# An adding transfer in place of a vector sum: S1 of a seven-product weight chunk made by DMA in the raw buffer

## The chip, the core and the metric

The kernel runs on one core of one Trainium2 chip. The metric is the device time of one execution in microseconds. Engines are named as in the profile: PE (matrix products), PEld (its weight loads), DVE (vector), ACT (scalar), POOL (GpSimd) and SP (which only issues transfers here).

## The reference, cut to what matters

A two-layer decoder trunk on 512 tokens of width 1024. Each layer is a mixer between two half-step SwiGLU feed-forward blocks, so there are four feed-forward blocks in all:

```
def swiglu(h, w_gate, w_up, w_down):
    return (jax.nn.silu(h @ w_gate) * (h @ w_up)) @ w_down

for i in range(2):
    x = x + 0.5 * swiglu(rmsnorm(x, ffn1_norm[i]), ffn1_w_gate[i], ffn1_w_up[i], ffn1_w_down[i])
    x = x + mixer_i(rmsnorm(x, mix_norm[i]))          # gated linear attention, then stick-breaking attention
    x = x + 0.5 * swiglu(rmsnorm(x, ffn2_norm[i]), ffn2_w_gate[i], ffn2_w_up[i], ffn2_w_down[i])
return rmsnorm(x, final_norm)
```

w_gate and w_up are 1024 x 2816, w_down is 2816 x 1024, all in float32.

## The kernel before, in words

Activations lie with features on partitions, tokens along the free dimension. Every float32 factor is split into a high part rounded to fp32r and a low part that is the rest; a product is three matrix products, high x high, low x high and high x low. The split of a weight is one copy on ACT (L138) and one subtraction on DVE (L139), in `Entry.split`.

A feed-forward block walks over 11 chunks of 256 columns of w_gate and w_up. From the third chunk on (9 of w_gate and 9 of w_up in each block, 72 in all) a chunk is a "seven-product" chunk: its 1024 x 256 block is read as a 2 x 2 matrix of blocks and multiplied with the 2 x 2 blocks of the activations by Strassen-Winograd, in seven products of 12 matrix products each instead of eight. In the tile `t` of a raw chunk (128 x 8 x 256) the blocks are A11 = `t[:, 0:4, 0:P]`, A21 = `t[:, 0:4, P:]`, A12 = `t[:, 4:8, 0:P]`, A22 = `t[:, 4:8, P:]`. The weights need four sums:

- S1 = A21 + A22 (L704) and S2 = S1 − A11 (L705), made by `sums_12` in one tile of 1024 columns and split as one unit;
- S3 = A11 − A21 (L710) and S4 = A12 − S2 (L711), made by `sums_34` likewise.

A chunk has two entries in the feed's queue, `body_1` (products with A11, S1, S2 and A12) and `body_2` (S3, S4, A22). After the product with A11 ACT copies the result from ps_w to ps_z (L746), and only then may PE go on in ps_w. The results go out through ACT copies (L749, L752, L764), DVE sums (L765, L769) and the gate: for w_gate a Silu on ACT (L729), for w_up a product on DVE (L732).

`Feed.start` sets the order of the work: at each entry it splits up to three entries ahead (no more than four full-size units), makes the sums of up to four entries, and loads the chunks of up to six. A load (L105) is one transfer of 1 MB issued by SP into one of two "raw" buffers; it waits until the buffer's last reader is done. Loads of down weights (`rawd`) stand in the same SP queue. A sum is made when its entry comes into view, so the first reader of a raw chunk on DVE is S1. Each engine works its instructions off in the order in which they were written.

Between the seven-product chunks stand the down products: `down` (results ps_d, in part copied by ACT at L340 and added onto the residual by a POOL-issued adding transfer, x<-d, L341) and `seven_down` (L374 to L445, with its own sums S1 to S4 from `rawd`, its own copies into ps_z at L408 and its additions onto the residual at L396).

Of the kernel before, what the change touches and what calls it, by code (L numbers as in the profile page):

```python
# [10 lines left out]
F32 = mybir.dt.float32  # L11
# [4 lines left out]
ALU = mybir.AluOpType  # L16
PSUM = bass.MemoryType.PSUM

P = 128
T = 512  # L20
D = 1024
KD = D // P
# [8 lines left out]
def turns(t):  # L31

    return t.rearrange("p (two n) -> p n two", two=2)


def flat(ps):

    return ps.rearrange("p (n two) -> p two n", two=2)


def pair(t):

    return t.rearrange("p (two n) -> p two n", two=2)
# [3 lines left out]
def decoder(ctx: ExitStack, tc: tile.TileContext, a: dict, out: bass.AP):  # L47
    nc = tc.nc
# [12 lines left out]
    def psum(name, tag=None):  # L61
        if tag is None:
            tag = order[turn_[0] % 8]
            turn_[0] += 1
        return pp.tile([P, T], F32, tag=tag, bufs=banks[tag], name=name)
# [25 lines left out]
    class Chunk:  # L91
        def __init__(self, src, n, m):
            self.src, self.n, self.m, self.t = src, n, m, None
            self.pool = None
            self.few = False

        def load(self):
            if self.t is None:
                if self.pool is not None:
                    self.t = self.pool.tile([P, self.n, self.m], F32, tag="raw0", bufs=4, name="raw0")  # L100
                elif self.few:
                    self.t = st["few"].tile([P, self.n, self.m], F32, tag="rawd", bufs=2, name="rawd")
                else:
                    self.t = wp.tile([P, self.n, self.m], F32, tag="raw", bufs=2, name="raw")
                nc.sync.dma_start(self.t, self.src)  # L105
            return self.t

    class Entry:
# [504 lines left out]
    class FFN:  # L613
# [80 lines left out]
        def seven(self, ch, group=None):  # L694

            H = T // 2
            s12, v = [None], {}  # L700

            def sums_12(t):
                s = s12[0] = self.tp.tile([P, KD, P], F32, tag="s", bufs=4, name="s12")
                nc.vector.tensor_tensor(out=s[:, 0:4], in0=t[:, 0:4, P:], in1=t[:, 4:8, P:], op=ALU.add)  # L704
                nc.vector.tensor_tensor(out=s[:, 4:8], in0=s[:, 0:4], in1=t[:, 0:4, 0:P], op=ALU.subtract)  # L705
                return s

            def sums_34(t):
                s = self.tp.tile([P, KD, P], F32, tag="s", bufs=4, name="s34")
                nc.vector.tensor_tensor(out=s[:, 0:4], in0=t[:, 0:4, 0:P], in1=t[:, 0:4, P:], op=ALU.subtract)  # L710
                nc.vector.tensor_tensor(out=s[:, 4:8], in0=t[:, 4:8, 0:P], in1=s12[0][:, 4:8], op=ALU.subtract)  # L711
                return s

            def prod(o, w, w0, b, first=True, c0=0):
                for j in range(4):
                    bh, bl = (turns(t) for t in b(j))
                    wh, wl = (t[:, w0 + j, c0 : c0 + P] for t in w)
                    for n, (l_, r_) in enumerate(((wh, bh), (wl, bh), (wh, bl))):
                        st["pe"] = nc.tensor.matmul(  # L719
                            o, l_, r_, start=first and j + n == 0, stop=j == 3 and n == 2, skip_group_check=True  # L720
                        ).ins

            def half(k0, c):
                return lambda j: (st["h"][k0 + j][:, c * H : c * H + H], st["l"][k0 + j][:, c * H : c * H + H])

            def gate(o, c, t):

                if group is None:
                    st["silu"] = nc.scalar.activation(pair(o[:, c : c + H]), t, AF.Silu).ins  # L729
                else:  # L730
                    g = self.gates[0 if o is v["o"][0] else 1]
                    nc.vector.tensor_tensor(  # L732
                        out=pair(o[:, c : c + H]), in0=t, in1=pair(g[:, c : c + H]), op=ALU.mult
                    )

            def body_1(W):


                a11, s, a2 = W
                v["a2"] = a2  # L740
                v["w"], v["q"] = psum("ps_w"), psum("ps_q")
                z = psum("ps_z")[:, 0:H]
                w, q = (v[n][:, 0:H] for n in "wq")
                o0, o1 = v["o"] = [self.tp.tile([P, T], F32, tag="t", name=n) for n in ("o0", "o1")]
                prod(w, a11, 0, half(0, 0))
                nc.scalar.copy(z, w)  # L746
                yield
                prod(q, s, 0, lambda j: self.t_half(0, j))
                nc.scalar.copy(pair(o1[:, H:T]), flat(q))  # L749
                yield  # L750
                prod(w, s, 4, lambda j: self.t_half(1, j), first=False)
                nc.scalar.copy(pair(o0[:, H:T]), flat(w))  # L752
                yield
                prod(z, a2, 0, half(4, 0), first=False)
                gate(o0, 0, flat(z))
                yield

            def body_2(W):
                (s,) = W
                w, q = (v[n][:, 0:H] for n in "wq")  # L760
                o0, o1 = v["o"]
                prod(w, s, 0, lambda j: self.t_half(2, j), first=False)
                u3 = self.tp.tile([P, H], F32, tag="c", bufs=1, name="u3")
                nc.scalar.copy(pair(u3), flat(w))  # L764
                nc.vector.tensor_tensor(out=o1[:, H:T], in0=u3, in1=o1[:, H:T], op=ALU.add)  # L765
                yield
                prod(q, s, 4, half(4, 1), first=False)
                oh = pair(o0[:, H:T])
                nc.vector.tensor_tensor(out=oh, in0=flat(q), in1=oh, op=ALU.add)  # L769
                gate(o0, H, oh)  # L770
                if group is not None:
                    close_0(o0)
                gate(o1, H, pair(o1[:, H:T]))
                yield
                prod(w, v["a2"], 0, lambda j: self.t_half(3, j), first=False, c0=P)
                gate(o1, 0, flat(w))
                if group is not None:
                    close_1(o0, o1)
                    del self.gates[:2]
                else:  # L780
                    self.gates += [o0, o1]
                yield

            def close_0(o0):
                if group in self.DOWN_SEVEN:
                    self.close_first(o0, group)
                else:
                    self.close(o0, group)

            def close_1(o0, o1):  # L790
                if group in self.DOWN_SEVEN:
                    self.close_second(o0, o1, group)
                else:
                    self.close(o1, group)


            units = [(ch, lambda t: t[:, 0:4, 0:P], 4, P), (ch, sums_12, KD, P), (ch, lambda t: t[:, 4:8], 4, 256)]
            feed.q.append(Entry(units, body_1))
            feed.q.append(Entry([(ch, sums_34, KD, P)], body_2))

        def t_half(self, i, j):
# [1112 lines left out]
```

## Time and profile before

| | |
|---|---|
| median of 3 runs | 1779.24 us (1779.19 to 1779.93) |
| the profiled execution's own time | 1779.44 us |
| its span | 1777.5 us |
| PE, DVE, ACT, POOL busy | 1756.3, 1508.6, 1081.6, 58.4 us |
| granted clock of TensorE | 0.999 |
| DMA | 193.93 MB, mean 109 GB/s |

The profile is of one execution. Busy time is the union of an engine's instructions; a group of instructions is given as line, engine, operation, output<-inputs, shapes and count, then busy us in all and mean ns of one, and after the second bar the idle time of that engine just before them with what ended it. Matrix products overlap one another, so their mean duration is longer than their distance. A timeline row has start, duration, engine, line and operands. A DMA row ends with the median time from issue to landing.

### The profile page before, as it was taken

How to read it: one execution, taken by the hardware profiler on the slowest of the kernel's cores; microseconds unless marked ns; L12 is line 12 of the kernel's file. 1: busy time of each engine (PE TensorE's matmuls, PEld its weight loads, DVE VectorE, ACT ScalarE, POOL GpSimd, SP SyncE). 2: the span in 40 equal slices, each digit the busy share in tenths (PEclk: the TensorE clock that was granted, in tenths of full speed). 3: DMA queues.
4: the chain of work that ended last, by engine and by line, in shares of the span. 5: the costliest groups of instructions: out<-in, count | busy, mean ns of one | idle time of the engine just before them, and what ended most of it. 6: DMA issues, size and time to landing. Idle time of an engine off the chain costs nothing.

```text
span 1777.5 us, 31388 instructions
## 1 busy us (share of the span) xinstructions
PE 1756.3 (99%) x12714; PEld 1630.4 (92%) x12714; DVE 1508.6 (85%) x2471; ACT 1081.6 (61%) x1886; POOL 58.4 (3%) x80
## 2 busy tenths in 40 slices
PE   9999999999999999999999999999999999999998
PEld 8999999889888899999889999999888888999997
DVE  8999797786888989888798988967898679997985
ACT  7556556554655556555565555555889745665655
POOL 0000000200000000000000000010000000000000
PEclk9999999999999999999999999999999999999999
DMA  5543435422123433344424344342212134434342
GB/s 168 153 120 118 125 103 148 112 72 72 49 95 95 130 108 119 119 119 126 141 85 130 103 124 135 110 120 83 84 49 78 66 95 131 131 108 129 114 131 65
DMA packets 186820, 193.93 MB, mean 109 GB/s; under 512 B 4978, under 2 KB 171172, under 8 KB 186676
## 3 DMA queue, kind: packets, MB, share of 16 engines
q1 hardware_dynamic: 177760, 175.91, 31.7%
q0 software_dynamic: 8672, 15.74, 4.9%
q8 instruction: 99, 1.62, 0.4%
q14 instruction: 45, 0.37, 0.1%
q10 hardware_dynamic: 244, 0.29, 0.0%
HBM read 175.17 MB, written 2.10 MB: 100 GB/s over the span
## 4 chain that ended last, share of the span: by engine, by line
PE 67%; DVE 22%; ACT 5%; DMA 3%; issue 3%; POOL 0%; DVEq 0%; SPq 0%; ACTq 0%; POOLq 0%
PE ps_w L719 16%; PE ps_d L80 11%; PE ps_q L719 8%; PE ps_f L80 7%; DVE wl L139 5%; PE ps_t L80 4%; PE ps_z L719 4%; PE ps_w L390 4%; PE ps_b L80 3%; PE ps_q L390 2%; ACT wh L138 2%; DMA raw<-in_ffn_w_gate_dram 1%; DVE ts L826 1%; PE ps_z L1402 1%; DVE nl L817 1%
## 5 line engine op out<-in xcount | busy, mean ns | idle before, releaser
L139 DVE TENSOR_TENSOR wl<-raw,wh 128x1024 fp32r<-128x1024 f32 x241 | 255.0, 1059 | 59.8 <-ACT wh L138 59.1
L138 ACT CAST wh<-raw 128x1024 fp32r<-128x1024 f32 x241 | 221.7, 921 | 77.1 <-PE ps_f L80 22.6
L139 DVE TENSOR_TENSOR wl<-s,wh 128x1024 fp32r<-128x1024 f32 x176 | 214.3, 1218 | 47.2 <-ACT wh L138 47.2
L719 PE MATMUL ps_w<-th,wh 128*128 128x256 f32 x864 | 239.4, 277 | 4.2 <-ACT ps_z L746 4.1
L719 PE MATMUL ps_w<-th,wl 128*128 128x256 f32 x864 | 237.6, 275 | 0.0
L719 PE MATMUL ps_w<-tl,wh 128*128 128x256 f32 x864 | 237.6, 275 | 0.0
L138 ACT CAST wh<-s 128x1024 fp32r<-128x1024 f32 x176 | 184.1, 1046 | 69.1 <-DVE s L705 19.3
L719 PEld LDWEIGHTS ps_w<-th,wh 128*128 128x128 f32 x864 | 165.8, 192 | 7.6 <-ACT ps_z L746 7.6
L80 PE MATMUL ps_f<-xh,wh 128*128 128x512 f32 x432 | 166.4, 386 | 0.0
L719 PEld LDWEIGHTS ps_w<-tl,wh 128*128 128x128 f32 x864 | 165.9, 192 | 0.0
L719 PEld LDWEIGHTS ps_w<-th,wl 128*128 128x128 f32 x864 | 165.8, 192 | 0.0
L80 PE MATMUL ps_f<-xh,wl 128*128 128x512 f32 x432 | 164.2, 380 | 0.5 <-DVE wl L139 0.5
L80 PE MATMUL ps_f<-xl,wh 128*128 128x512 f32 x432 | 163.9, 379 | 0.0
L80 PE MATMUL ps_d<-hl,wh 128*128 128x512 f32 x416 | 158.0, 380 | 1.7 <-DVE hl L817 1.7
L80 PE MATMUL ps_d<-hh,wh 128*128 128x512 f32 x416 | 158.0, 380 | 0.5 <-ACT hh L816 0.5
L80 PE MATMUL ps_d<-hh,wl 128*128 128x512 f32 x416 | 157.7, 379 | 0.0
L139 DVE TENSOR_TENSOR wl<-rawd,wh 128x1024 fp32r<-128x1024 f32 (+1 forms) x100 | 96.0, 963 | 16.0 <-ACT wh L138 15.8
L138 ACT CAST wh<-rawd 128x1024 fp32r<-128x1024 f32 (+1 forms) x100 | 82.8, 845 | 39.3 <-PE ps_d L80 25.6
L341 POOL DMA_DIRECT2D x<-d x56 | 48.6, 879 | 1531.1 <-ACT d L340 829.9
L80 PEld LDWEIGHTS ps_f<-xl,wh 128*128 128x128 f32 x432 | 81.6, 189 | 11.5
L80 PEld LDWEIGHTS ps_f<-xh,wl 128*128 128x128 f32 x432 | 81.7, 189 | 11.3 <-DVE wl L139 0.9
L80 PEld LDWEIGHTS ps_f<-xh,wh 128*128 128x128 f32 x432 | 81.7, 189 | 10.8
(355 smaller groups left out, 5324.9 us busy)
## 6 DMA issues: line engine op xcount, KB each, us to landing
raw<-in_ffn_w_gate_dram SPq DMA_DIRECT2D x43, 1024.0 KB, 5.5
raw<-in_ffn_w_up_dram SPq DMA_DIRECT2D x43, 1024.0 KB, 5.4
rawd<-in_ffn_w_down_dram SPq DMA_DIRECT2D x84, 512.0 KB, 3.7
x<-d POOLq DMA_DIRECT2D x56, 256.0 KB, 4.6
raw<-in_gla_w_in_dram SPq DMA_DIRECT2D x12, 1024.0 KB, 5.3
raw<-in_sb_w_in_dram SPq DMA_DIRECT2D x16, 512.0 KB, 3.8
raw<-in_gla_w_out_dram SPq DMA_DIRECT2D x4, 1024.0 KB, 5.0
raw<-in_sb_w_in_dram SPq DMA_DIRECT2D x4, 1024.0 KB, 5.2
```

What stands on the lines that cost most here:

```text
L80: st["pe"] = nc.tensor.matmul(ps, l, r, start=first, stop=last).ins
L138: st["cut"] = nc.scalar.copy(h[:, k], part).ins
L139: nc.vector.tensor_tensor(out=l[:, k], in0=part, in1=h[:, k].bitcast(F32), op=ALU.subtract)
L341: nc.gpsimd.dma_start(xs[k], d, accum_op=ALU.add)
L390: st["pe"] = nc.tensor.matmul(ps, l_, r_, start=first and c + n == 0, stop=c == 1 and n == 2, skip_group_check=True).ins
L719: st["pe"] = nc.tensor.matmul(o, l_, r_, start=first and j + n == 0, stop=j == 3 and n == 2, skip_group_check=True).ins
L817: nc.vector.tensor_tensor(out=l, in0=t, in1=h.bitcast(F32), op=ALU.subtract)
L826: nc.vector.tensor_tensor(out=o, in0=p, in1=q, op=ALU.subtract)
L1402: nc.tensor.matmul(o_, l_, r_, start=first, stop=last, skip_group_check=True)
```

## The change

In the 72 seven-product chunks of w_gate and w_up, once a chunk's load has landed, a transfer issued by POOL adds A22 onto A21 in the raw buffer (256 KB, from on-chip memory to on-chip memory, four runs of 512 bytes in each partition). S1 is then no tile of its own: it is split straight from the raw chunk. S2 is made from it by one subtraction, S3 as A22 − S2 and S4 as A12 − S2. The unit of S1 and S2 is split in two pieces, S1 from the raw chunk and S2 from its own tile, which is half as wide. `seven_down` stays as it was.

```
         def load(self):
...
                 nc.sync.dma_start(self.t, self.src)
+                if self.onto is not None:
+                    o, i = self.onto(self.t)
+                    nc.gpsimd.dma_start(o, i, accum_op=ALU.add)
             return self.t
...
             s12, v = [None], {}
+            ch.onto = lambda t: (t[:, 0:4, P:], t[:, 4:8, P:])
 
             def sums_12(t):
-                s = s12[0] = self.tp.tile([P, KD, P], F32, tag="s", bufs=4, name="s12")
-                nc.vector.tensor_tensor(out=s[:, 0:4], in0=t[:, 0:4, P:], in1=t[:, 4:8, P:], op=ALU.add)
-                nc.vector.tensor_tensor(out=s[:, 4:8], in0=s[:, 0:4], in1=t[:, 0:4, 0:P], op=ALU.subtract)
-                return s
+                s = s12[0] = self.tp.tile([P, 4, P], F32, tag="s", bufs=4, name="s2")
+                nc.vector.tensor_tensor(out=s, in0=t[:, 0:4, P:], in1=t[:, 0:4, 0:P], op=ALU.subtract)
+                return t[:, 0:4, P:], s
 
             def sums_34(t):
                 s = self.tp.tile([P, KD, P], F32, tag="s", bufs=4, name="s34")
-                nc.vector.tensor_tensor(out=s[:, 0:4], in0=t[:, 0:4, 0:P], in1=t[:, 0:4, P:], op=ALU.subtract)
-                nc.vector.tensor_tensor(out=s[:, 4:8], in0=t[:, 4:8, 0:P], in1=s12[0][:, 4:8], op=ALU.subtract)
+                for i, two in enumerate((slice(P, 2 * P), slice(0, P))):
+                    nc.vector.tensor_tensor(
+                        out=s[:, 4 * i : 4 * i + 4], in0=t[:, 4:8, two], in1=s12[0], op=ALU.subtract
+                    )
                 return s
```

More of the change, by code (lines that the diff above doesn't have):

```diff
@@ L95, in __init__ @@
             self.few = False
+            self.onto = None
         def load(self):
```

## The prediction

> **What bounds the kernel now.** I read the page's busy shares first, then busy time by stretch, then groups by line and shape, the DMA issues, and last the timeline of single engines around one chunk.
>
> ```profile
> span 1777.5 us, 31388 instructions
> PE 1756.3 (99%) x12714; PEld 1630.4 (92%) x12714; DVE 1508.6 (85%) x2471; ACT 1081.6 (61%) x1886; POOL 58.4 (3%) x80
> ```
>
> PE idles 1777.5 − 1756.3 = 21.2 us of the whole span. That is all that any relief of another engine can win; a wait that reaches PE is lost in full. DVE at 85% looks like a distant second, but the average misleads:
>
> ```profile
> core 0: us, PE busy (x) PEld busy (x) DVE busy (x) ACT busy (x) POOL busy (x), PEclk, DMA share, GB/s
> 650.00:700.00 50.00, 49.84 (x422) 48.82 (x421) 49.06 (x84) 30.35 (x55) 0.86 (x1) 1.00 0.37 111
> ```
>
> Inside the seven-product stretches DVE is busy 49.06 of 50 us beside PE's 49.84. There both are full, and DVE, whose order is fixed, cannot make up a wait.
>
> **What the change removes and adds on the engines.** Each of the 72 seven-product chunks loses one DVE sum (S1), and its S1/S2 split becomes two pieces of 512 in place of one of 1024, on ACT and on DVE. S2, S3 and S4 stay one 512-wide DVE operation each.
>
> ```profile
> L704 DVE TENSOR_TENSOR s<-raw 128x512 f32<-128x512 f32 x72 | 49.1, 682 | 2.2 <-DMA raw<-in_ffn_w_gate_dram 2.2
> L139 DVE TENSOR_TENSOR wl<-s,wh 128x1024 fp32r<-128x1024 f32 x176 | 214.3, 1218 | 47.2 <-ACT wh L138 47.2
> ```
>
> These durations overlap their neighbours, so I price by distance between starts, from DVE's timeline around one chunk (its gate-weight load was issued at 140.31):
>
> ```profile
> 145.67 0.68 DVE L139 TENSOR_TENSOR wl<-raw,wh 128x512 fp32r<-128x512 f32 x1
> 146.27 0.68 DVE L704 TENSOR_TENSOR s<-raw 128x512 f32<-128x512 f32 x1
> 146.87 0.68 DVE L710 TENSOR_TENSOR s<-raw 128x512 f32<-128x512 f32 x1
> 147.47 0.68 DVE L705 TENSOR_TENSOR s<-s,raw 128x512 f32<-128x512 f32 x1
> 148.07 0.68 DVE L374 TENSOR_TENSOR s<-rawd 128x512 f32<-128x512 f32 x1
> 148.68 1.21 DVE L139 TENSOR_TENSOR wl<-raw,wh 128x1024 fp32r<-128x1024 f32 x1
> 149.81 0.68 DVE L711 TENSOR_TENSOR s<-raw,s 128x512 f32<-128x512 f32 x1
> 150.41 0.42 DVE L765 TENSOR_TENSOR o<-u,o 128x256 f32<-128x256 f32 x1
> ```
>
> A 512-wide operation occupies DVE 0.60 us (145.67 to 146.27), a 1024-wide one 1.13 (148.68 to 149.81). Saved per chunk: 0.60 − (2 × 0.60 − 1.13) = 0.53 us, over 72 chunks 38 us of DVE. By itself this brings almost nothing, as PE is the bound.
>
> ACT's timeline in the same chunk:
>
> ```profile
> 150.87 0.42 ACT L729 ACTIVATE o<-o 128x256 f32<-128x256 f32 x1 [1.75 <-DVE o L765]
> 151.19 1.03 ACT L138 CAST wh<-s 128x1024 fp32r<-128x1024 f32 x1
> 152.13 0.41 ACT L729 ACTIVATE o<-o 128x256 f32<-128x256 f32 x1
> 152.45 0.36 ACT L729 ACTIVATE o<-ps_w 128x256 f32<-128x256 f32 x1
> 152.71 1.03 ACT L138 CAST wh<-s 128x1024 fp32r<-128x1024 f32 x1
> 153.65 0.37 ACT L746 COPY ps_z<-ps_w 128x256 f32<-128x256 f32 x1
> 153.95 0.62 ACT L138 CAST wh<-raw 128x512 fp32r<-128x512 f32 x1
> 154.47 0.37 ACT L749 COPY o<-ps_q 128x256 f32<-128x256 f32 x1
> ```
>
> One 1024 copy takes 0.94 us from start to start (152.71 to 153.65), one of 512 takes 0.52 (153.95 to 154.47): + 0.10 us per chunk. ACT's idle 39% hides it, except where it stands directly ahead of the copy into ps_z (L746) in a chunk that is late; 36 such chunks (counted below) make 3.6 us.
>
> **What the change adds in latency.** DVE's first touch of a chunk used to need only the load. Now S2 (and ACT's copy of A21+A22) needs load, then an issue on POOL, then 256 KB added from SBUF onto SBUF. No row of before shows this transfer; the nearest is x<-d, also adding, also 256 KB, also from POOL:
>
> ```profile
> raw<-in_ffn_w_gate_dram SPq DMA_DIRECT2D x43, 1024.0 KB, 5.5
> raw<-in_ffn_w_up_dram SPq DMA_DIRECT2D x43, 1024.0 KB, 5.4
> x<-d POOLq DMA_DIRECT2D x56, 256.0 KB, 4.6
> DMA to landing us min/median/max: 3.3/4.6/8.4
> L341 POOL DMA_DIRECT2D x<-d x56 | 48.6, 879 | 1531.1 <-ACT d L340 829.9 <-DVE tl L817 485.3 <-DVE x L396 179.2
> L1013 POOL DMA_DIRECT2D gr<-in_gla_w_in_dram x1 | 1.2, 1217 | 0.0
> ```
>
> The fourth row is x<-d's own (L341): 3.3 at least, 4.6 in the middle, 8.4 at most. The new transfer has runs of 512 bytes, four per partition, where x<-d has one of 2 KB; gr, with eight runs per partition, took POOL 1.22 us against 0.88, so the runs cost up to some 0.3 us there. Against that it starts just when its own chunk's load has left the queues. I take 4.6, and keep 3.3 and 6.5 (half way from 4.6 to 8.4) as ends. The Trainium skill, page "DMA: Bandwidth & Descriptors", section "Anatomy of one DMA — SWDGE (gpsimd) path", fits a POOL-issued transfer as 2.0 us plus bytes at 436 GB/s, an estimate of 2.6 us here. The trace disagrees for transfers that add: none of the 56 landed under 3.3.
>
> In the built program S2 stands in DVE's order where S1 stood, ahead of the same evacuations; PE's order is unchanged. So how early DVE came to S1 decides. SP's issues of raw loads, with DVE's S1 of the same chunks (the chunk issued at 140.31 has its S1 above, at 146.27):
>
> ```profile
> 42.97 0.37 SPq L105 DMA_DIRECT2D raw<-in_ffn_w_gate_dram  x1
> 64.29 0.37 SPq L105 DMA_DIRECT2D raw<-in_ffn_w_gate_dram  x1
> 140.31 0.37 SPq L105 DMA_DIRECT2D raw<-in_ffn_w_gate_dram  x1
> 149.92 0.37 SPq L105 DMA_DIRECT2D raw<-in_ffn_w_up_dram  x1
> 1694.41 0.37 SPq L105 DMA_DIRECT2D raw<-in_ffn_w_up_dram  x1
> ...
> 54.04 0.68 DVE L704 TENSOR_TENSOR s<-raw 128x512 f32<-128x512 f32 x1
> 71.38 0.69 DVE L704 TENSOR_TENSOR s<-raw 128x512 f32<-128x512 f32 x1 [0.68 <-DMA raw<-in_ffn_w_gate_dram]
> 156.46 0.68 DVE L704 TENSOR_TENSOR s<-raw 128x512 f32<-128x512 f32 x1
> 1700.95 0.69 DVE L704 TENSOR_TENSOR s<-raw 128x512 f32<-128x512 f32 x1
> ```
>
> Pairing all 72 this way, 36 are tight: first 64.29 to 71.38, last 1694.41 to 1700.95, from 6.0 to 9.0 us, 7.31 on average. The other 36 have 11.1 or more (42.97 to 54.04 is one of 11.1). Load plus transfer is 5.4 + 4.6 = 10.0: the loose chunks hide it, the tight ones miss it by 10.0 − 7.31 = 2.7 us on average.
>
> **How much of that reaches PE.** Take the chunk issued at 140.31. Its sum now lands at 150.3, so S2 starts 4.0 us after S1 did. Queued behind S2 on DVE are S3, S4, the A2 split and then L765, for which ACT's L729 waits, and behind that on ACT stand two splits, two more gates and the copy into ps_z. From S1 to L765 DVE had 150.41 − 146.27 = 4.14 us of work; in the changed order it is S2, S3, S4 and one 1024 split, 3 × 0.60 + 1.13 = 2.93, as S1 is gone and L374 now follows L765. So L765 comes at 150.3 + 2.9 = 153.2, or 2.8 late: 1.2 us is covered. L746 is late by the same, and PE has nothing in hand there, because it waited for that copy already:
>
> ```profile
> PEld ps_w L719 <- ACT ps_z L746: 7.6, 18, 1.4
> SPq L105 <- DVE wl L139: 1100.5, 129, 27.5
> ```
>
> The second row says that raw loads wait for DVE splits to free their buffer: a late DVE also issues the load after next late (and the down-weight loads queued behind it on SP). Two tight chunks in a row therefore turn in a loop of S2, split, load, add: 0.6 + 1.1 + 5.4 + 4.6 = 11.7 us, where S1 to S1 took 156.46 − 146.27 = 10.2. That is 1.5 us instead of the 2.3 that the cover rule gives its second chunk (10.0 − 6.5 − 1.2); others, with less work ahead of L765, have less cover, and I let these balance.
>
> On POOL the new issue waits at its head for the raw load, and x<-d is queued behind it; in the built order the adding transfer for a chunk stands ahead of x<-d issues that come later anyway, so I put nothing down for that. Not covered by anything: DVE's and ACT's queues behind S2.
>
> **The sum.** Each tight pair costs what it lacks to 10.0 − 1.2 = 8.8 us: 36 × (8.8 − 7.31) = 54 us (four pairs at 9.0 cost nothing, which moves it by 0.8). With ACT's 3.6 us it is 58. The profiled execution took 1779.44 us (span 1777.5 and 1.9 around it), against a median of 1779.24. Forecast: 1779.4 + 58 = **1837 us**.
>
> **Rivals.**
> *Mostly hidden.* The transfer lands at x<-d's shortest, 3.3. The limit is then 5.4 + 3.3 − 1.2 = 7.5, 24 pairs fall short, by 17 us in all: 1797. For it: PE needs the split weights of S1 only later, for the chunk with S1 at 146.27 here,
>
> ```profile
> 162.21 0.28 PE L719 MATMUL ps_q<-th,wh 128*128 128x256 f32 x1
> ```
>
> so only the evacuations queued behind S2 hurt. Against it: 3.3 is the minimum of 56. Chance of 1797 or less without a gain 0.07, of which 0.03 within 0.2% (3.6 us, about what a measurement can tell from no change). By the skill's 2.6 us the limit would be 6.8 and the loss 5 us.
> *Faster.* The sum lands before DVE comes to S2, and the 0.53 us per chunk bring ACT's copy into ps_z forward, which ends PE's 7.6 us of waiting for it: 1772. It decides only if load plus add stays under the shortest pairs, 6.0 us plus the cover of 1.2, so the add under 1.8 us. Nothing in the trace is near it. Chance 0.06.
> *Much slower.* The add takes 7 us (runs of 512 bytes, down-weight loads beside it, POOL longer): 36 × (12.4 − 1.2 − 7.31) = 140, or 1923 with ACT. x<-d's maximum of 8.4 speaks for it, its median against. Chance above 1905: 0.10.
> *Nothing changes* because the scheduler puts S2 later: the built order excludes it.
>
> **Numbers.** The forecast's case, 1797 to 1905, has 0.77. The low end is the 3.3 us add (+ 17); the high end the 6.5 us one: 36 × (11.9 − 1.2 − 7.31) = 122 and 4 make 1905. Left out: 0.06 + 0.07 below, 0.10 above, though part of the second lies at the edge. Slower: 0.77 + 0.10 + 0.04 = 0.91; same 0.03; faster 0.06.
>
> **What would show it.** In the changed profile: 72 POOL issues raw<-raw of 256 KB landing in some 4.6 us; DVE's S2 idle before it by some 36 × 2.7 = 97 us in all, less what DVE's later arrival takes off, named after that DMA; PE idle grown from 21 to about 80 us, put down to ACT's copies into ps_z (L746 and L408); DVE busy down by some 38 us. If S2 idles but PE does not, the cover is bigger than I hold; if S2 hardly idles, the add is shorter; if the waits stand on ACT's copy of A21+A22 and not on S2, the order of blame is wrong.

## The result, and the profile after

The changed kernel took 1892.88 us in the median of six runs (1884.48 to 1894.88), against 1779.22 for the kernel before beside it: a ratio of 1.063, with an interval of 1.061 to 1.065. It is 114 us slower, where 58 was forecast. In code the changed lines lie four to six further down: L138 and L139 are now L142 and L143, S2 is L709, S3 and S4 are L715, L390 is L394, L408 is L412, L719 is L725, L729 is L735, L746 is L752, L765 is L771, and the new transfer is L109. The copy that makes hh on ACT, L816, is L822. In some of the experiments these lines shift by a few more.

The page of after, its first lines, and the view of span and clock:

```profile
span 1892.3 us, 31697 instructions
PE 1794.2 (95%) x12714; PEld 1659.8 (88%) x12714; DVE 1477.9 (78%) x2471; ACT 1091.0 (58%) x1958; POOL 151.8 (8%) x152
core 0: 1892.3 us, clock 0.980
```

The span grew by 1892.3 − 1777.5 = 114.8 us, and two terms make it up. PE's idle time is 1892.3 − 1794.2 = 98.1 us in place of 21.2: 76.9 more. And PE was *busy* 1794.2 − 1756.3 = 37.9 us longer with exactly the same 12714 products. The clock says why: 0.980 in place of 0.999 over 1892.3 us is 36 us of lost work. The first term was forecast at about 58, the second at nothing.

The groups of after and its DMA issues (the last line is the landing time of L109, least, median and most):

```profile
L109 POOL DMA_DIRECT2D raw<-raw x72 | 92.9, 1290 | 1133.7 <-DVE wl L143 846.8 <-DMA raw<-in_ffn_w_up_dram 116.2 <-DVE hl L823 46.9
L709 DVE TENSOR_TENSOR s<-raw 128x512 f32<-128x512 f32 x72 | 49.8, 691 | 130.9 <-issue 93.9 <-DMA raw<-raw 37.0
raw<-raw POOLq DMA_DIRECT2D x72, 256.0 KB, 4.3
DMA to landing us min/median/max: 4.2/4.3/7.9
```

The transfer lands in 4.3 us (4.6 was taken), and DVE stands idle 130.9 us ahead of S2, where S1 had stood 2.2. One tight chunk and its successor show the path. The timeline of after, engine by engine: SP's loads, POOL's adding transfers, DVE, ACT, PE.

```profile
157.52 0.37 SPq L106 DMA_DIRECT2D raw<-in_ffn_w_gate_dram  x1
169.61 0.37 SPq L106 DMA_DIRECT2D raw<-in_ffn_w_up_dram  x1
...
163.47 1.28 POOL L109 DMA_DIRECT2D raw<-raw  x1 [20.65 <-DVE wl L143]
175.52 1.28 POOL L109 DMA_DIRECT2D raw<-raw  x1 [10.77 <-DVE wl L143]
...
167.75 0.69 DVE L709 TENSOR_TENSOR s<-raw 128x512 f32<-128x512 f32 x1 [4.12 <-issue]
168.36 1.22 DVE L143 TENSOR_TENSOR wl<-raw,wh 128x1024 fp32r<-128x1024 f32 x1
169.50 1.29 DVE L715 TENSOR_TENSOR s<-raw,s 128x512 f32<-128x512 f32 x2
170.70 0.42 DVE L771 TENSOR_TENSOR o<-u,o 128x256 f32<-128x256 f32 x1
179.76 0.69 DVE L709 TENSOR_TENSOR s<-raw 128x512 f32<-128x512 f32 x1 [2.96 <-issue]
...
171.16 0.42 ACT L735 ACTIVATE o<-o 128x256 f32<-128x256 f32 x1 [4.94 <-DVE o L771]
174.02 0.37 ACT L752 COPY ps_z<-ps_w 128x256 f32<-128x256 f32 x1
...
174.44 0.38 PE L725 MATMUL ps_w<-th,wh 128*128 128x256 f32 x1 [3.28 <-ACT ps_z L752]
```

Read downwards: load issued at 157.52, POOL's issue at 163.47, S2 4.28 us later at 167.75, after 4.12 us of idle DVE. Behind it in DVE's order comes L771 at 170.70, which releases ACT's gate (4.94 us idle); behind that on ACT comes the copy into ps_z, and PE starts after 3.28 us of waiting for it. The bracket names "issue" where the chain does not name the transfer; the distance of 4.28 us from POOL's issue, beside a median landing of 4.3, does. Late DVE also issues the next load late, at 169.61, and the second S2 follows the first by 179.76 − 167.75 = 12.0 us.

The waits of after (engine, what waits, for whom: us in all, times, longest), and then the two rows of before that answer to the first and the third, L729 and L719:

```profile
ACT o L735 <- DVE o L771: 101.4, 36, 8.9
PE ps_w L394 <- ACT ps_z L412: 36.8, 16, 4.9
PE ps_w L725 <- ACT ps_z L752: 34.0, 17, 7.2
PE ps_d L80 <- ACT hh L822: 8.8, 5, 2.5
ACT wh L142 <- DMA raw<-raw: 20.3, 4, 5.7
```

```profile
ACT o L729 <- DVE o L765: 49.6, 32, 3.0
...
PE ps_w L719 <- ACT ps_z L746: 4.1, 10, 1.2
```

PE's waits for the two copies into ps_z are 36.8 + 34.0 = 70.8 us, where before had 4.1: 66.7 of the 76.9 us of added idle time. Most of the rest is PE's wait for hh, a copy behind ACT's own wait for the transfer (last row). In 33 places this is 2.1 us at a time, and that size matters for the second term. The next views show PE's weight loads just behind the wait above (timeline of after), and busy time by stretch (columns as in the prediction; the clock stands behind POOL):

```profile
174.44 0.19 PEld L725 LDWEIGHTS ps_w<-th,wh 128*128 128x128 f32 x1 [3.47 <-ACT ps_z L752]
174.55 0.19 PEld L725 LDWEIGHTS ps_w<-th,wl 128*128 128x128 f32 x1
...
176.29 0.33 PEld L725 LDWEIGHTS ps_z<-nh,wh 128*128 128x128 f32 x1
176.50 0.33 PEld L725 LDWEIGHTS ps_z<-nh,wl 128*128 128x128 f32 x1
```

```profile
175.90:179.30 3.40, 3.40 (x19) 3.40 (x18) 0.90 (x2) 1.32 (x2) 0.90 (x1) 0.50 0.68 77
150.00:200.00 50.00, 39.94 (x336) 39.37 (x336) 36.13 (x62) 25.50 (x51) 3.84 (x3) 0.96 0.45 112
```

PE first goes on at full speed, one load each 0.11 us; from 175.9 for 3.4 us the granted clock is 0.50 and a load takes its turn each 0.21 us. The trace of after has 16 such stretches, of 3.4 or 6.8 us, 71.7 us in all; half of that is 36 us. The trace of before has none, and no wait of PE over 2 us. (Each trace has one more at its very end, behind PE's last product, which costs nothing and is left out.)

### The profile page after: what moved, and what is told of

The parts are those of the page before. It is cut to its first block, busy times and chain, and to the rows that moved or that the text cites. A ratio compares the mean times of both kernels' runs of the same rounds, so it can differ in the third digit from the quotient of the medians.

```text
span 1892.3 us, 31697 instructions
## 1 busy us (share of the span) xinstructions
PE 1794.2 (95%) x12714; PEld 1659.8 (88%) x12714; DVE 1477.9 (78%) x2471; ACT 1091.0 (58%) x1958; POOL 151.8 (8%) x152
## 3 DMA queue, kind: packets, MB, share of 16 engines
q8 instruction: 99, 1.62, 0.4%
## 4 chain that ended last, share of the span: by engine, by line
PE 56%; DVE 20%; DMA 10%; issue 8%; ACT 6%; POOL 0%; POOLq 0%; DVEq 0%; ACTq 0%; SPq 0%
PE ps_d L80 12%; PE ps_w L725 11%; PE ps_f L80 8%; DVE wl L143 7%; PE ps_q L725 5%; PE ps_t L80 4%; DMA raw<-in_ffn_w_gate_dram 4%; DMA raw<-raw 3%; PE ps_z L725 3%; PE ps_w L394 3%; PE ps_b L80 3%; ACT wh L142 2%; DMA raw<-in_ffn_w_up_dram 2%; DVE s L715 1%; PE ps_z L1408 1%
## 5 line engine op out<-in xcount | busy, mean ns | idle before, releaser
L143 DVE TENSOR_TENSOR wl<-raw,wh 128x1024 fp32r<-128x1024 f32 (+1 forms) x313 | 303.3, 976 | 89.4 <-ACT wh L142 88.0
L142 ACT CAST wh<-raw 128x1024 fp32r<-128x1024 f32 (+1 forms) x313 | 266.2, 851 | 137.1 <-PE ps_f L80 22.6
L725 PE MATMUL ps_w<-th,wh 128*128 128x256 f32 x864 | 241.6, 280 | 34.2 <-ACT ps_z L752 34.0
L725 PE MATMUL ps_w<-tl,wh 128*128 128x256 f32 x864 | 239.8, 278 | 0.0
L725 PE MATMUL ps_w<-th,wl 128*128 128x256 f32 x864 | 239.7, 277 | 0.0
L725 PEld LDWEIGHTS ps_w<-th,wh 128*128 128x128 f32 x864 | 167.6, 194 | 37.9 <-ACT ps_z L752 37.8
L143 DVE TENSOR_TENSOR wl<-s,wh 128x1024 fp32r<-128x1024 f32 (+1 forms) x176 | 176.4, 1002 | 24.1 <-ACT wh L142 24.0
L109 POOL DMA_DIRECT2D raw<-raw x72 | 92.9, 1290 | 1133.7 <-DVE wl L143 846.8
L142 ACT CAST wh<-s 128x1024 fp32r<-128x1024 f32 (+1 forms) x176 | 153.1, 870 | 43.6 <-PE ps_q L725 17.2
L725 PEld LDWEIGHTS ps_w<-tl,wh 128*128 128x128 f32 x864 | 167.9, 194 | 0.0
L725 PEld LDWEIGHTS ps_w<-th,wl 128*128 128x128 f32 x864 | 167.7, 194 | 0.0
L709 DVE TENSOR_TENSOR s<-raw 128x512 f32<-128x512 f32 x72 | 49.8, 691 | 130.9 <-issue 93.9
L143 DVE TENSOR_TENSOR wl<-rawd,wh 128x1024 fp32r<-128x1024 f32 (+1 forms) x100 | 96.1, 964 | 16.1 <-ACT wh L142 16.0
L142 ACT CAST wh<-rawd 128x1024 fp32r<-128x1024 f32 (+1 forms) x100 | 82.7, 843 | 32.5 <-PE ps_d L80 17.6
L80 PEld LDWEIGHTS ps_d<-hh,wh 128*128 128x128 f32 x416 | 80.4, 193 | 21.4 <-ACT hh L822 10.8
L715 DVE TENSOR_TENSOR s<-raw,s 128x512 f32<-128x512 f32 x144 | 96.5, 687 | 0.8
```

The costliest lines, as they stand in the source:

```text
L80: st["pe"] = nc.tensor.matmul(ps, l, r, start=first, stop=last).ins
L109: nc.gpsimd.dma_start(o, i, accum_op=ALU.add)
L142: st["cut"] = nc.scalar.copy(h[:, k], part).ins
L143: nc.vector.tensor_tensor(out=l[:, k], in0=part, in1=h[:, k].bitcast(F32), op=ALU.subtract)
L709: nc.vector.tensor_tensor(out=s, in0=t[:, 0:4, P:], in1=t[:, 0:4, 0:P], op=ALU.subtract)
L715: nc.vector.tensor_tensor(out=s[:, 4 * i : 4 * i + 4], in0=t[:, 4:8, two], in1=s12[0], op=ALU.subtract)
```

## The experiments

"Base" below is the first experiment, from which the others that keep a DVE sum are built.

**The sum without the transfer.** In place of the transfer, DVE adds in the raw chunk:

```
-            ch.onto = lambda t: (t[:, 0:4, P:], t[:, 4:8, P:])
             def sums_12(t):
+                nc.vector.tensor_tensor(out=t[:, 0:4, P:], in0=t[:, 0:4, P:], in1=t[:, 4:8, P:], op=ALU.add)
```

> The changed kernel, but DVE adds A22 onto A21 in the raw chunk itself (one 512-wide operation, just ahead of S2) and there is no adding transfer; the split in two pieces, S3 from A22 and S2, and the order stay. Waiting theory (all of the 114 us comes from S2 and what queues behind it waiting for load plus transfer): back to 1777 to 1784 us, DVE busy up by some 40 us, no half-clock stretches. Rival, the two-piece split and the new order cost themselves: stays over 1800.

Measured: 1785.49 us, ratio 1.0028 (1.0015 to 1.0040), a little over the 1777 to 1784 expected; DVE's busy time rose by 39.8 us, as expected. Its busy times, and its span and clock:

```profile
PE 1760.1 (99%) x12714; PEld 1634.8 (92%) x12714; DVE 1517.7 (85%) x2543; ACT 1090.8 (61%) x1958; POOL 58.4 (3%) x80
core 0: 1785.2 us, clock 0.997
```

The new splits and forms of S2 to S4 cost 5 to 6 us in all (5.4 against the kernel before run beside it). PE idles 1785.2 − 1760.1 = 25.1 us, and the clock was low in two stretches of 3.4 us, both near the start of a block, where none was expected. The other 107 us belong to the transfer.

**Loose places only, tight places only.** Of the 18 seven-product chunks of a block, nine keep the transfer and nine take DVE's sum:

```
+            nth = self.nth = getattr(self, "nth", -1) + 1
+            if nth in (0, 1, 3, 4, 5, 6, 11, 13, 14):          # loose; tight: (2, 7, 8, 9, 10, 12, 15, 16, 17)
                 ch.onto = lambda t: (t[:, 0:4, P:], t[:, 4:8, P:])
```

> Adding transfer only in the nine of 18 chunks of each block that had 11.1 us or more from load issue to S1 before (places 0, 1, 3 to 6, 11, 13, 14); the other nine add on DVE in place. Waiting theory: the 36 transfers are hidden, 1776 to 1788 us. Rival, a transfer costs by its traffic and by POOL whether or not it is awaited: half of the 114 us stays, some 1836.

> The complement: adding transfer only in places 2, 7 to 10, 12 and 15 to 17 of each block, DVE add in the others. Waiting theory: nearly the whole loss, 1870 to 1895 us, PE idle some 80 to 100 us and half-clock stretches as in the changed kernel. Traffic rival: some 1836.

Measured: loose 1795.76 us (ratio 1.0087, 1.0072 to 1.0102), tight 1901.26 (1.0681, 1.0662 to 1.0699). Against the base the 36 loose ones cost 10 us, the 36 tight ones 116. So the prediction's division by the distance from load to S1 holds, and the loose ones come out 8 us over the 1776 to 1788 expected; two rows of the loose kernel's waits show where:

```profile
ACT wh L142 <- DMA raw<-raw: 21.2, 4, 6.0
PE ps_d L80 <- ACT hh L826: 8.4, 4, 2.9
```

Four times, once in each block, ACT waits for the transfer at its own copy of A21+A22: 5 us each, at the same four places as in the row of 20.3 us of after. Behind it on ACT stands the copy that makes hh, and PE waits for that. This is the prediction's own sign that its order of blame is wrong, in these four places: it had not looked at the start of a block. The tight version, with 1870 to 1895 expected, is even 8 us slower than all 72 transfers. It carries DVE's sum in the other half, but why that costs so much was not followed up.

**A shorter wait.** POOL adds by itself instead of issuing a transfer:

```
-                    nc.gpsimd.dma_start(o, i, accum_op=ALU.add)
+                    nc.gpsimd.tensor_tensor(out=o, in0=o, in1=i, op=ALU.add)
```

> The changed kernel with the adding transfer replaced by one vector add on POOL (A21 += A22, 128 x 512, in the raw chunk, issued at the same place of the queue). POOL's memset of that size took 0.53 to 0.83 us, so I expect 1 to 2 us for the add. Waiting theory: load plus add is 7 to 7.5 us, below the 8.8 at which a pair starts to cost, so 1774 to 1788 us, a little better than before if DVE's 38 us are worth anything. Rival, POOL and DVE hinder one another when both read the on-chip memory: DVE's two-input operations get longer than 684 ns for 512 columns, and the time stays over 1795.

Measured: 1817.19 us, ratio 1.0204 (1.0189 to 1.0219). POOL's group, two rows of the waits, and the clock:

```profile
L109 POOL TENSOR_TENSOR raw<-raw 128x512 f32<-128x512 f32 x72 | 182.7, 2537 | 1013.6 <-DMA raw<-in_ffn_w_gate_dram 686.0 <-DMA raw<-in_ffn_w_up_dram 149.0 <-DVE wl L143 144.8
DVE s L709 <- POOL raw L109: 30.8, 24, 2.5
PE ps_w L725 <- ACT ps_z L752: 24.2, 18, 2.8
core 0: 1815.7 us, clock 0.997
```

The 1774 to 1788 of the waiting theory was missed; the time lies where the rival put it, over 1795. POOL's addition takes 2.54 us on average (1.64 in the median, 7.9 at most), some 1.8 us less than the transfer. The rival's sign is there too: S2 takes 713 ns and S3 and S4 720, against 691 and 687 in after, and DVE is busy 1512.7 us in all, 34.8 more than in after with as many instructions. DVE waits 30.8 us for POOL, and 24.2 us appear at PE, 15.3 more than in the base. Waiting and hindrance are mixed in this run, so it does not show how much of a wait is covered. PE idles in 39 places for over 0.3 us, but only once for over 2 us, and the clock is low in only two stretches of 3.4 us: short waits mostly leave it alone.

**Four waits, and the same four filled.** Only place 8 keeps the transfer, four in all; then, in a second kernel, place 7 also runs 26 products whose result nobody reads, where PE would wait:

```
+            if nth in (8,):
                 ch.onto = lambda t: (t[:, 0:4, P:], t[:, 4:8, P:])
...
+                if nth in (7,):                                # second kernel only
+                    ps = psum("ps_j")[:, 0:H]
+                    for n in range(26):
+                        st["pe"] = nc.tensor.matmul(
+                            ps, a11[0][:, n % 4, 0:P], turns(half(0, 0)(n % 4)[0]), start=n == 0, stop=n == 26 - 1
+                        ).ins
```

> Adding transfer only in place 8 of the 18 chunks of each block (four transfers in all), DVE add in place in the other 68: the base is the kernel with all adds on DVE, 1785.5 us. It gives the price of one wait. Theory A (the wait costs PE's idle time and, as the idle time is over 2 us, a stretch of half clock after it): four times 3.0 to 3.3 idle and 1.7 clock, 1803 to 1807 us, with three or four half-clock stretches of 3.4 us more than the base. Theory B (idle time alone counts, the lower clock in the changed kernel has another cause): 1797 to 1799, no more half-clock stretches than the base. Theory C (one wait alone is taken up by later slack, only the row of them hurts): under 1790.

> The one above, and in place 7 of each block PE has 26 further matrix products (2.9 us) of no use between the product with S1 and the one that waits for ACT's copy into ps_z, into a PSUM tile that nobody reads: they fill the idle time that the wait makes. Theory A: the half-clock stretches of the waits go away and the idle time turns into busy time, 5 to 8 us less than without the filling, some 1798. Theory B: the same time as without it, or some us more where the filling is longer than the wait.

Measured: 1800.55 us (ratio 1.0123, 1.0108 to 1.0139) and, filled, 1792.07 (1.0071, 1.0058 to 1.0083). Busy time and clock of the one and of the other:

```profile
PE 1765.7 (98%) x12714; PEld 1640.7 (91%) x12714; DVE 1515.9 (84%) x2539; ACT 1091.5 (61%) x1958; POOL 63.6 (4%) x84
core 0: 1798.8 us, clock 0.993
```

```profile
PE 1768.7 (99%) x12818; PEld 1642.4 (92%) x12818; DVE 1514.6 (85%) x2539; ACT 1091.6 (61%) x1958; POOL 63.3 (4%) x84
core 0: 1790.1 us, clock 0.999
```

Four waits cost 15 us beside the base, 3.8 each: 8.0 us of PE idle (33.1 against 25.1) and 5.6 of PE busy with the same products. That lies between the times of theories A and B; the clock is low in five stretches, three more than in the base, as A said. The filled kernel decides: it has 104 products more, about 104 × 0.11 = 11 us of work, and is 8.5 us *faster* (5 to 8 expected), its clock back at 0.999. Its four transfers are there, and DVE waits for them as long as without the filling (17.1 us and 16.8). So it is PE's waits, not anything in the transfer's traffic, that bring the low clock.

The Trainium skill, page "TensorE: Matmul & The Clock Gate", section "What's actually happening", says the clock is halved after an idle window of about 3.4 us, a window of 3413 ns that runs freely and does not start anew with a kernel; the stretches of 3.4 and 6.8 us here agree. Its section "HAM oscillation — how this bites in real kernels" gives the rule of no idle gap above about 3.4 us; here shorter ones sufficed. Counted over all twelve traces of this case (PE idle for over 0.3 us, after the first 20 us; "low" where a stretch of half clock began in the gap or up to 3.6 us behind it):

| PE idle, us | gaps | followed by low clock |
|---|---|---|
| under 1 | 175 | 6 |
| 1 to 2 | 73 | 7 |
| 2 to 2.5 | 18 | 11 |
| 2.5 to 3.5 | 38 | 34 |
| over 3.5 | 16 | 15 |

The traces also show why a gap of 2 to 2.5 us only sometimes does it. All stretches of one trace begin a whole number of 3.413 us apart: in after three of them begin at 87.156, 175.902 and 199.795 us, 26 and 7 times 3.413 us apart. Cut into windows on this grid, the twelve traces have 6231 windows at full clock (after the first 20 us). In 60 of them PE idled for 2.00 us or more in all, and each of the 60 was followed by half clock; of ten with 1.85 to 2.00 us six were, and of the other 6161 one (with 1.62). A window at half clock was followed by another one in all 12 cases with 0.6 us or more of idle time, and by full clock in all 67 with less. So what counts in these traces is PE's idle time within one window of the grid, not the length of a gap. In the kernel with four waits a gap of 2.36 us at 627.2 put 2.31 us into one window and drew a stretch; in the filled one a gap of 2.41 us at 624.5 was divided into 1.27 and 1.14 and drew none. That stretch, 1.7 of the 8.5 us, went by chance and not by the filling.

**Filling in the changed kernel.** 24 such products in places 1, 7, 8, 15 and 16 of each block of the changed kernel:

> The changed kernel with 24 such useless products (2.7 us) in places 1, 7, 8, 15 and 16 of each block, 20 spots, 54 us of PE work in all; the waits in the down products stay unfilled. Theory A: half-clock time falls from 71 us to 20 to 40, PE idle falls by some 45; the time is 1870 to 1890. Theory B: 1893 or above, up to 1945 if the spots were not idle.

Measured: 1923.47 us, ratio 1.0807 (1.0792 to 1.0821); 1870 to 1890 was expected, a miss. Busy times, clock, and PE's waits for the two copies into ps_z:

```profile
PE 1838.3 (96%) x13194; PEld 1704.3 (89%) x13194; DVE 1477.9 (77%) x2471; ACT 1092.4 (57%) x1958; POOL 151.9 (8%) x152
core 0: 1918.0 us, clock 0.987
PE ps_w L394 <- ACT ps_z L412: 39.0, 16, 3.5
PE ps_w L726 <- ACT ps_z L753: 8.4, 8, 5.0
```

The clock rose to 0.987 as it should, and the waits in the seven-product chunks went from 34.0 to 8.4 us. Those in `seven_down` (36.8 before, 39.0 now) stayed, and 480 products at 0.11 us are 53 us of added work. For them PE's idle time fell by 18.4 us (98.1 to 79.7; 45 were expected) and the half-clock time from 71.7 to 47.8 us, worth 12. This filling cost more than it won.

**The wait made shorter by an earlier half.** The load of a chunk in two halves, right columns first, so that the transfer waits for the first half alone:

```
+                    nc.sync.dma_start(self.t[:, :, P:], self.src[:, :, P:])
+                    nc.sync.dma_start(self.t[:, :, 0:P], self.src[:, :, 0:P])
```

> The changed kernel, but the load of a seven-product chunk is two transfers, first its right 128 columns (A21 and A22, 512 KB), then the left ones, and the add waits for the first alone. The first half should land some 3.7 us after its issue (512 KB of down weights took 3.7), so load plus add is some 8.6 us instead of 10.3. Waiting theory: the loss falls with it, between the POOL add (8.1 us, 1817) and the changed kernel (10.3 us, 1893): 1825 to 1845. Rival (the add is late for another cause than the load ahead of it, such as POOL's queue): 1880 to 1895.

Measured: 1839.33 us, ratio 1.0333 (1.0318 to 1.0347), as expected. The landing time of the first half (least, median, most), the group of S2, and the clock:

```profile
DMA to landing us min/median/max: 3.9/4.1/5.9
L713 DVE TENSOR_TENSOR s<-raw 128x512 f32<-128x512 f32 x72 | 49.5, 687 | 75.5 <-DMA raw<-raw 39.4 <-issue 35.8 <-DVE wl L147 0.2
core 0: 1836.6 us, clock 0.993
```

The first half lands in 4.1 us in place of 5.4, DVE's idle time ahead of S2 falls from 130.9 to 75.5, and the kernel gains 53.5 us on the changed one. With 1.3 us less in the path, 36 tight chunks gain 1.5 us each. Of the 55.7 us between the two profiled spans, 34.9 are PE's idle time (98.1 to 63.2), 1.0 for each tight chunk, and 20.8 are PE's busy time, with 20.5 us of half clock in place of 71.7.

**The transfers without the wait.** The kernel before, with the same 72 transfers issued behind S3, when A21 has no reader left:

```
                 nc.vector.tensor_tensor(out=s[:, 4:8], in0=t[:, 4:8, 0:P], in1=s12[0][:, 4:8], op=ALU.subtract)
+                nc.gpsimd.dma_start(t[:, 0:4, P:], t[:, 4:8, P:], accum_op=ALU.add)
                 return s
```

> The kernel before, with S1 and S2 on DVE as they were, and after S3 the same 72 transfers (A22 added onto A21, 256 KB in runs of 512 bytes), whose result nobody uses any more: the traffic, the packets and the POOL issues of the change without its wait before S2. Only the next load into that buffer waits for them, and it waits for a later split anyway. If the cost of the change is the wait (theory): 1779 to 1784 us, no half-clock stretch, loads still 5.4 to 5.9 us. If it is contention of the added packets with loads and down weights, or DVE and ACT slowed while they land (rival): a large part of the 114 us, over 1810.

Measured: 1800.87 us, ratio 1.0108 (1.0092 to 1.0123): neither the 1779 to 1784 of the theory nor the rival's 1810. The loads' landing, two rows of the waits (SP's and DVE's), and the clock:

```profile
raw<-in_ffn_w_gate_dram SPq DMA_DIRECT2D x43, 1024.0 KB, 5.4
raw<-in_ffn_w_up_dram SPq DMA_DIRECT2D x43, 1024.0 KB, 5.5
SPq L105 <- DMA raw<-raw: 331.2, 49, 15.1
DVE s L704 <- DMA raw<-in_ffn_w_gate_dram: 14.6, 5, 4.0
core 0: 1798.8 us, clock 0.995
```

Loads land as fast as before (5.5 and 5.4), and DVE and ACT are busy 1509.2 and 1081.9 us for 1508.6 and 1081.6, so the added traffic slows nothing there. The smaller loads of down weights do land later, in 4.0 us for 3.7 (4.3 in after); what that costs, if anything, is not shown apart. But 49 loads now wait for a transfer to leave their buffer; the expectation had said a later split would hold it longer anyway, which is wrong. At the start of each block such a load comes late, DVE waits up to 4.0 us, and PE has four waits of 2.5 to 4.0 us, each with 3.4 us of half clock. The 21 us are again waits and their clock: idle 34.1 (12.9 more), busy 8.4 more.

**Only where there is room.** The kernel before, with the changed sums and the transfer in places 1, 3, 5, 11 and 13 of each block alone, the 20 loosest:

> The kernel before everywhere except in places 1, 3, 5, 11 and 13 of each block (20 chunks of 72, those with 15 us or more from load issue to S1), which use the changed sums with the transfer. All that is bought is 20 x 0.53 = 11 us of DVE. Theory (PE bounds the kernel, DVE's time is worth nothing): 1777 to 1783, no difference that can be told. Rival (DVE bounds the dense stretches and its relief reaches PE): 1770 or less. If these chunks wait for the transfer as well: 1785 or more.

Measured: 1778.47 us, ratio 0.9992 (0.9983 to 1.0001), no difference, as expected. Its busy times:

```profile
PE 1755.3 (99%) x12714; PEld 1630.2 (92%) x12714; DVE 1499.9 (84%) x2471; ACT 1085.3 (61%) x1906; POOL 84.5 (5%) x100
```

DVE is relieved by 1508.6 − 1499.9 = 8.7 us, and the time stands still. No version tried beats the kernel before by more than can be told.

## Why the prediction was right, and where its size was off

*The bound.* Right. PE sets the time, and what DVE saves is worth nothing: 30.7 us less of DVE in after (38 forecast), 8.7 in the last experiment, whose time shows no gain from it.

*ACT's longer split.* 0.10 us per chunk was forecast. ACT's busy time rose by 1091.0 − 1081.6 = 9.4 us, 0.13 per chunk. The base, which holds it and no transfer, is 5 to 6 us slower for 3.6 forecast; these are not divided further.

*The latency.* The sum of load and transfer was 10.0 us. In the chunk shown it is 167.75 − 157.52 = 10.23: the transfer itself is shorter than x<-d's 4.6, but POOL's issue starts some 0.6 us after the load's 5.4 are over (157.52 + 5.4 = 162.9, issue at 163.47), a step that the sum left out. (Over the 60 chunks whose landing the trace has, this step is 0.56 us in the median.) The Trainium skill's estimate of 2.6 us, from the section of "DMA: Bandwidth & Descriptors" that the prediction names, does not hold for transfers that add: the least of 72 is 4.2.

*Who waits.* Right, name by name, in the tight chunks: S2, then L771 (2.95 us behind S2, 2.93 forecast), ACT's gate, the copy into ps_z, PE. The loop of two tight chunks turns in 12.0 us for 11.7. DVE's idle ahead of S2 is 130.9 us in 40 waits, for 97 in 36: 0.2 us more latency on each of 36 gives 105, and the rest are longer waits, among them a few in places that had counted as loose.

*The cover.* Too large. It was 1.2 us; in the chunk shown DVE waits 4.12 us and PE 3.28, so 0.84 is covered. With the two sizes measured in this chunk the prediction's own rule gives 36 × (10.23 − 0.84 − 7.31) = 75 us, and PE's idle time grew by 76.9. That these agree so well is partly chance: over all 36 tight places load to S2 took from 10.0 to 15.6 us, 10.3 in the median and 10.9 on average, and some 10 of the 76.9 us are PE's waits for hh and its low part hl (8.8 + 3.2 for 0.5 + 1.7 in before), which the sum did not have. The prediction had seen that other chunks have less cover and let that balance; it did not.

*The missing term.* The sum took a wait of PE at its own length. A wait of 2 us or more mostly draws a stretch of half clock behind it (60 of 72 in the table), since most of it falls into one window of 3.4 us, and this was 36 to 38 of the 114 us. Nothing in the profile of before could show its size, since PE never waited over 2 us there; but the forecast wait of 1.5 us on average, with 2.8 in its own example, was near enough to ask. With 75, 38 and ACT's 3.6 the sum, step by step, gives 117 for 114.8 measured between the spans.

*The range.* That 1893 lies within 1797 to 1905 is in part luck. The high end stood for a transfer of 6.5 us; the transfer took 4.3, and the clock, which the range did not hold, filled the room. With the measured 5.4 + 0.6 + 4.3 us, the forecast's cover of 1.2 and no clock the sum gives 36 × (9.1 − 7.31) = 64, and with ACT's 3.6 the time would be 1847.

*The rivals.* Hidden and faster fell with the landing time of 4.3 us. "Much slower" named a transfer of 7 us; the time went two thirds of the way there, from 1837 to 1923, by another road.

## What to carry to other kernels

Moving a sum into the DMA puts a second latency, here 0.6 + 4.3 us, behind every load, and it is free only where the buffers hold the data that much ahead; count the slack chunk by chunk, not on average. When PE is the bound, price a new wait twice: its length, and the half-speed stretch that comes when some 2 us of it fall into one window of 3.4 us, here half as much again. Relief of an engine that is not the bound pays for neither.

## What was not expected of the hardware

The half clock came after idle times of 2.0 to 2.5 us in 11 of 18 cases, and stood for 3.4 us or twice that; by windows of a fixed grid of 3.413 us, it came in 60 of 60 cases with 2.00 us or more of idle time in one window. An addition of two 128x512 float32 operands took POOL 2.54 us on average and 1.64 in the median, where DVE takes 0.68, and beside it DVE's own took 713 to 720 ns.
